# Spreading the value steps of the second stick-breaking group over three slots of a two-layer attention kernel

## The chip, the cores and the metric

The kernel runs on one core of a Trainium2 chip. The metric is the device time of one execution in microseconds, taken as the median over several runs; lower is better.

## The reference

The program is an encoder trunk of two layers (DEPTH = 2) on 512 tokens of width 1024. Each layer projects the residual stream once and feeds two mixers of eight heads each: group A, stick-breaking attention, and group B, sparse attention over each query's top 128 keys. The change touches the values of group A alone:

```python
def hybrid_layer(x, w_in, w_out, ln_g, ln_b, rel_bias, topk):
    proj = jnp.einsum('bsd,dn->bsn', x, w_in)
    qA, kA, vA, gA, qB, kB, vB, gB, qI, kI, wI = jnp.split(proj, SPLIT_POINTS, axis=-1)
    oA = stick_breaking_attention(heads(qA), heads(kA), heads(vA))
    oB = dsa_sparse_attention(heads(qB), heads(kB), heads(vB), ..., rel_bias, topk)
    mix = jnp.concatenate([oA * jax.nn.silu(gA), oB * jax.nn.silu(gB)], axis=-1)
    return layer_norm(ALPHA * x + jnp.einsum('bsm,md->bsd', mix, w_out), ln_g, ln_b)

# stick_breaking_attention, for s < t:
#   A[t,s] = sigmoid(z[t,s]) * prod_{s<j<t} (1 - sigmoid(z[t,j]));  out = A @ v
```

## The kernel before

Every product of float32 operands is made of three products of halves: a high half (a rounded copy made by ScalarE) and a low half (the source minus the high half, made by VectorE or GpSimd). So every operand that TensorE reads has such a pair of steps behind it. `XH`, `XL` are the halves of the layer's input; `whi`, `wlo` those of a weight piece. A weight piece `raw` is loaded by a transfer that SyncE issues, copied to `whi` by ScalarE in one instruction (L212) and subtracted to `wlo` by GpSimd in four or two (L215). Two `raw` buffers and four `whi`/`wlo` pairs turn over.

A layer is a loop over 91 slots (`s`). A slot starts one task, a block of 128 queries of one head: tasks 0 to 23 are the indexer's, 24 to 55 those of the eight stick heads (four blocks of a head, with 128, 256, 384 and 512 keys, in turn), then those of group B. A stick task goes through stages in consecutive slots: its logits `z` (TensorE, L517 and L520) and the sigmoid `om` (ScalarE, L704) in its own slot; a scan along the keys (VectorE, L709) one slot later; the transposes into `tr` (TensorE, L525), the high copy into one `AT` tile (ScalarE, L714) and the low copy into another (VectorE, L717) three slots later. When the four blocks of a head have been through that, the slot after the last one runs the eight matmuls of the head's output `o` (L692), which read the two `AT` tiles and the values `vt`. Its second reads are of the low tile. The output is then copied and added up (`mixt`, L594 and L596) and multiplied into `M` by GpSimd (L597). Between these, TensorE is filled with projection matmuls (`pj`, L266 to L268, and `pjv`), ahead of their use, by a table of slots by which each unit must be done. VectorE also runs the top-k rounds (L841, L842) in the same slots, and the gates' products (`sig`, L581 and L584), which GpSimd multiplies into `M` (L582, L585).

The order of the instructions on each engine is the order in which the code is written: PE, ACT, DVE and POOL each run their own list in that order and wait at an instruction until its inputs are there.

The scan makes the sum of a stick head a sum over differences of neighbouring value rows. So the values of a group go through extra steps: the projection is copied to `V_NOW`, shifted by one row into `V_PREV` by three transfers, then VectorE subtracts (L329, in place, the whole 128 x 1024; the trace names both tiles `M`, in which they lie), and the result is split into `vt`: two high copies on ScalarE (L346) and two low subtractions on VectorE (L344), each of half the token blocks.

These steps wait in a list `pending`. At the end of each slot `run_pending` takes one from every entry's count and runs entries from the front of the list while the front one's count is below zero. For the second stick group (heads 4 to 7, tasks 40 to 55), `project_v` appends an entry with count `SHIFT_SLOTS[1]` = 2, which calls `value_steps`. It falls due at the end of slot 41, in both layers. The first group's steps are called from elsewhere and the change leaves them alone. The values of the second group are read first by `o` of its first head, in slot 47. The `o` that runs in slot 43, soon after the steps, belongs to the last head of the first group and reads the other `vt`.

Of the kernel before, what the change touches and what calls it, by code (L numbers as in the profile page):

```python
# [102 lines left out]
def tile_hybrid(ctx: ExitStack, tc: tile.TileContext, xt, x, w_in, w_ki, w_out, ln_g, ln_b, rel_bias, onehot, out, depth=DEPTH):  # L103
# [182 lines left out]
    def project_v(l, unit, vt, keys=None):  # L286
# [9 lines left out]
        for tb in range(NTB):  # L296
            if tb:
                stream.want = i + min(tb + 1, 3) + (keys is not None)
            full = ppj.tile([P, S], F32, tag="pj", name="pjv")[:, :n]
            acc = full[:, :W256]  # L300
            for kc in range(KC):
                whi, wlo = (t[:, kc % 4, :] for t in w[kc // 4])
                T.matmul(full, XH[:, tb, kc, :], whi, start=kc == 0, stop=False)  # L303
                T.matmul(full, XL[:, tb, kc, :], whi, start=False, stop=False)  # L304
                T.matmul(full, XH[:, tb, kc, :], wlo, start=False, stop=kc == KC - 1)  # L305
                if kc == KC - 1:
                    if keys is not None:
                        later.append(lambda tb=tb, full=full: keep_keys(tb, full))
                    if unit[0] == "A":
                        later.append(lambda tb=tb, acc=acc: A.activation(V_NOW[:, tb, :], acc, AF.Copy))  # L310
                    else:
                        later.append(lambda tb=tb, acc=acc: evac_v(vv, tb, acc))
                if (tb, kc) == (NTB - 1, KC - 1) and unit[0] == "A":
                    later.append(shift_values)
                    pending.append([SHIFT_SLOTS[1], lambda: value_steps(vv)])
                yield 324 * n // W256
# [3 lines left out]
    pending = []  # L320
# [7 lines left out]
    def value_differences(engine, tbs=slice(0, NTB)):  # L328
        engine.tensor_tensor(V_PREV[:, tbs], V_PREV[:, tbs], V_NOW[:, tbs], ALU.subtract)  # L329

    def value_parts(vv):
        for i in range(4):
            value_part(vv, *divmod(i, 2))

    def value_steps(vv):
        value_differences(V)
        value_parts(vv)

    def value_part(vv, low, half):
        t = slice(2 * half, 2 * half + 2)  # L340
        src = V_PREV[:, t].rearrange("p t (h d) -> p t h d", d=HD)
        hi, lo = vv[:, t, :, :HD], vv[:, t, :, HD:]
        if low:
            V.tensor_tensor(lo, src, hi, ALU.subtract)  # L344
        else:
            A.activation(hi, src, AF.Copy)  # L346
# [785 lines left out]
```

## Time and profile before

| | before |
|---|---|
| median of 3 runs | 640.04 us (640.04 to 640.9) |
| the profiled execution | 639.84 us |
| its span, first to last instruction | 638.0 us |
| TensorE (PE) busy | 626.1 us, 98% |
| weight loads (PEld) busy | 546.7 us, 86% |
| VectorE (DVE) busy | 486.8 us, 76% |
| GpSimd (POOL) busy | 363.3 us, 57% |
| ScalarE (ACT) busy | 343.0 us, 54% |
| granted TensorE clock | 0.998 |

The profile gives, for each engine, the instructions in order of time, each with its start, its duration, its line and its tiles, and in brackets how long the engine had been idle before it and what ended that. The chain of waits is followed back from the last instruction to what released each step. Times in it count from the start of the span. Starts and ends on one engine can overlap by up to a tenth of a microsecond, and the ends of matmuls are modelled. The steps that the change moves lie near 135 us (layer 0) and near 449 us (layer 1).

### The profile page before, as it was taken

The page shows a single profiled execution, that of the slowest core. Times are in us where ns is not written, and L with a number is a line of the kernel's source. Part 1 is how long each engine was busy: PE and PEld are TensorE (multiplying, and loading weights), DVE is VectorE, ACT ScalarE, POOL GpSimd, SP SyncE. Part 2 cuts the span into 40 slices and gives each one's busy share as a digit, 9 for nine tenths or more (in the row PEclk, how much of TensorE's full clock was granted, in tenths as well). Part 3 has the DMA queues.
Part 4 walks back from the last instruction along what each step waited for, and adds up shares of the span by engine and source line. Part 5 has one row for each costly group of instructions (what it writes and reads, how often), then busy time and mean ns, then how long its engine had stood idle before and what let it go on. Part 6 is the DMA issues. An engine that isn't in the chain of part 4 may idle for free.

```text
span 638.0 us, 10261 instructions
## 1 busy us (share of the span) xinstructions
PE 626.1 (98%) x3501; PEld 546.7 (86%) x3501; DVE 486.8 (76%) x1058; ACT 343.0 (54%) x686; POOL 363.3 (57%) x380
## 2 busy tenths in 40 slices
PE   8999999999999999999999999999999999999995
PEld 7988888978889889988899888899788898898884
DVE  3778999988965775667845789999988576666677
ACT  5686555444357466883135855454444566678700
POOL 5463544448466676798134545535574587778721
PEclk9999999999999999999999999999999999999999
DMA  7624243312253475363314343333123724734402
GB/s 246 203 78 133 99 132 100 92 46 96 99 157 92 125 190 169 113 197 118 133 67 131 107 126 99 105 95 125 40 100 113 167 86 121 186 126 138 172 33 99
DMA packets 31779, 77.41 MB, mean 121 GB/s; under 512 B 6572, under 2 KB 10668, under 8 KB 31728
## 3 DMA queue, kind: packets, MB, share of 16 engines
q1 hardware_dynamic: 31440, 76.51, 39.0%
q8 instruction: 27, 0.44, 0.3%
q10 hardware_dynamic: 288, 0.26, 0.1%
q14 instruction: 24, 0.20, 0.1%
HBM read 61.84 MB, written 4.44 MB: 104 GB/s over the span
## 4 chain that ended last, share of the span: by engine, by line
PE 93%; DVE 3%; ACT 2%; issue 1%; DMA 1%; SPq 0%; POOL 0%; DVEq 0%; ACTq 0%
PE pj L266 15%; PE pj L267 15%; PE pj L268 15%; PE pjo L796 13%; PE o L692 6%; PE tr L525 5%; PE pjv L303 4%; PE pjv L304 4%; PE pjv L305 4%; PE z L520 4%; PE z L517 4%; PE pjv L427 2%; PE pjq L429 1%; PE trx L1050 1%; DMA q_raw<-in_w_in_dram 1%
## 5 line engine op out<-in xcount | busy, mean ns | idle before, releaser
L215 POOL TENSOR_TENSOR wlo<-raw,whi 128x256 fp32r<-128x256 f32 (+1 forms) x250 | 222.9, 922 | 162.2 <-ACT whi L212 161.4
L266 PE MATMUL pj<-XH,whi 128*128 128x512 f32 (+1 forms) x432 | 171.5, 397 | 0.0
L267 PE MATMUL pj<-XL,whi 128*128 128x512 f32 (+1 forms) x432 | 166.4, 385 | 0.0
L268 PE MATMUL pj<-XH,wlo 128*128 128x512 f32 (+1 forms) x432 | 166.2, 385 | 0.0
L268 PEld LDWEIGHTS pj<-XH,wlo 128*128 128x128 f32 x432 | 81.1, 188 | 16.1
L267 PEld LDWEIGHTS pj<-XL,whi 128*128 128x128 f32 x432 | 81.4, 188 | 12.2
L266 PEld LDWEIGHTS pj<-XH,whi 128*128 128x128 f32 x432 | 81.3, 188 | 12.2
L704 ACT ACTIVATE om<-z 128x128 f32<-128x128 f32 (+1 forms) x64 | 28.0, 438 | 111.5 <-PE z L520 61.1
L212 ACT ACTIVATE whi<-raw 128x1024 fp32r<-128x1024 f32 x78 | 81.9, 1055 | 7.4 <-DMA raw<-in_w_in_dram 7.0
L597 POOL TENSOR_TENSOR M<-M,mixt 64x512 f32<-64x512 f32 x24 | 40.6, 1691 | 51.6 <-DVE mixt L596 45.2
L709 DVE TENSOR_TENSOR_SCAN om<-om,future 128x128 f32<-128x128 f32 (+1 forms) x64 | 63.3, 988 | 0.2
L303 PE MATMUL pjv<-whi,XH 128*128 128x256 f32 x192 | 56.9, 296 | 0.0
L305 PE MATMUL pjv<-wlo,XH 128*128 128x256 f32 x192 | 54.2, 283 | 0.0
L304 PE MATMUL pjv<-whi,XL 128*128 128x256 f32 x192 | 54.2, 282 | 0.0
L841 DVE MAX8 m<-scores 128x8 f32<-128x256 f32 (+2 forms) x96 | 52.8, 550 | 0.1
L842 DVE MATCH_REPLACE8 scores<-m,scores 128x256 f32<-128x256 f32 (+2 forms) x96 | 52.1, 543 | 0.0
L692 PE MATMUL o<-AT,vt 128*128 128x512 f32 (+4 forms) x256 | 46.7, 323 | 2.8 <-ACT AT L714 2.7
L754 ACT ACTIVATE p<-p,mn 128x128 f32<-128x128 f32 (+1 forms) x64 | 35.8, 559 | 20.2 <-DVE mn L749 19.9
L692 PEld LDWEIGHTS o<-AT,vt 128*128 128x128 f32 (+1 forms) x256 | 36.5, 182 | 7.7 <-ACT AT L714 3.5
L520 PE MATMUL z<-k,q 128*128 128x128 f32 (+3 forms) x128 | 41.7, 326 | 0.0
L796 PE MATMUL pjo<-whi,XH 128*128 128x512 f32 (+1 forms) x118 | 41.1, 387 | 0.0
L796 PE MATMUL pjo<-wlo,XH 128*128 128x512 f32 (+1 forms) x118 | 41.1, 384 | 0.0
(165 smaller groups left out, 1282.4 us busy)
## 6 DMA issues: line engine op xcount, KB each, us to landing
raw<-in_w_in_dram SPq DMA_DIRECT2D x66, 512.0 KB, 3.3
k<-k SPq DMA_DIRECT2D x32, 256.0 KB, 5.6
raw<-in_w_out_dram SPq DMA_DIRECT2D x14, 512.0 KB, 3.2
gbias<-f_dram SPq DMA_DIRECT2D x18, 256.0 KB, 3.3
XN<-in_x_dram SPq DMA_DIRECT2D x8, 256.0 KB
y_dram<-XN SPq DMA_DIRECT2D x4, 512.0 KB, 2.6
XN<-y_dram SPq DMA_DIRECT2D x8, 256.0 KB, 3.7
M<-M SPq DMA_DIRECT2D x4, 448.0 KB
```

Source lines behind the costliest of these rows:

```text
L212: A.activation(hi, src, AF.Copy)
L215: low = lambda lo=lo[:, c], src=src[:, c], hi=hi[:, c]: lo_engine.tensor_tensor(lo, src, hi, ALU.subtract)
L266: T.matmul(o, w[0], XH[:, tb:, kc, :], start=first, stop=False)
L267: T.matmul(o, w[0], XL[:, tb:, kc, :], start=False, stop=False)
L268: T.matmul(o, w[1], XH[:, tb:, kc, :], start=False, stop=last)
L303: T.matmul(full, XH[:, tb, kc, :], whi, start=kc == 0, stop=False)
L304: T.matmul(full, XL[:, tb, kc, :], whi, start=False, stop=False)
L305: T.matmul(full, XH[:, tb, kc, :], wlo, start=False, stop=kc == KC - 1)
L520: T.matmul(self.z[:, :nn], c, d, start=False, stop=True)
L692: T.matmul(self.o[:m, sb * P :], vt[:, sb, self.hh * P : self.hh * P + m], at_block(self.at[j], sb, sb, NTB - sb), start=n == 0, stop=n == 7)
L709: V.tensor_tensor_scan(rev, rev, future[:, S - n :][:, ::-1], 1.0, ALU.mult, ALU.max)
L796: T.matmul(acc[:, cols], mixed[:, tb, m, :], w[:, cols], start=n == 0, stop=n == len(steps) - 1)
```

## The change

`value_steps` no longer runs the four parts behind the difference in the same slot. It appends four entries to `pending`: the two high copies with count 0, the two low subtractions with count 1. The entries are appended after the counts have been taken down for that slot, so the high copies run at the end of the next slot (42) and the low subtractions at the end of the one after it (43). No instruction is added or removed.

```diff
     def value_steps(vv):
         value_differences(V)
-        value_parts(vv)
+        for i in range(4):
+            pending.append([i // 2, lambda i=i: value_part(vv, *divmod(i, 2))])
```

The rows below are the order of the programs, layer 0; layer 1 moves alike. The file after is one line longer, so its lines from 338 on count one more. On ACT, before: behind the high copy of a three-block transpose come the two high copies of the values, then the copy of a weight piece (1569), then the sigmoid of 384 keys and the high copy of the four-block transpose.

```order
L714 ACTIVATE AT_107<-tr 128x3x128
L346 ACTIVATE vt<-M 128x8x64 x2
L212 ACTIVATE whi_1569<-raw_1404 128x1024
L704 ACTIVATE om<-z 128x384
L714 ACTIVATE AT_107<-tr 128x4x128
L704 ACTIVATE om<-z 128x512
```

On ACT, after (the same weight piece is now numbered 1565):

```order
L715 ACTIVATE AT_107<-tr 128x3x128
L212 ACTIVATE whi_1565<-raw_1404 128x1024
L705 ACTIVATE om<-z 128x384
L715 ACTIVATE AT_107<-tr 128x4x128
L347 ACTIVATE vt<-M 128x8x64 x2
L705 ACTIVATE om<-z 128x512
```

The values' copies moved behind the weight copy, one sigmoid and the four-block copy. On DVE, before: the difference and both low subtractions stand in front of the scan of 256 keys and the four-block low copy into `AT_108`.

```order
L842 MATCH_REPLACE scores_503<-m_1548,scores_503 128x256
L329 TENSOR_TENSOR M<-M 128x1024
L344 TENSOR_TENSOR vt<-M,vt 128x8x64 x2
L709 SCALAR_TENSOR_TENSOR om<-om,future 128x256
L717 SCALAR_TENSOR_TENSOR AT_108<-tr,AT_107 128x4x128
L841 MAX m_1591<-scores_504 128x8
L842 MATCH_REPLACE scores_504<-m_1591,scores_504 128x384
L709 SCALAR_TENSOR_TENSOR om<-om,future 128x384
L584 TENSOR_TENSOR sig<-pj,sig 128x512
```

On DVE, after, from the instruction that now follows the difference to the low subtractions:

```order
L710 SCALAR_TENSOR_TENSOR om<-om,future 128x256
L718 SCALAR_TENSOR_TENSOR AT_108<-tr,AT_107 128x4x128
L842 MAX m_1587<-scores_504 128x8
L843 MATCH_REPLACE scores_504<-m_1587,scores_504 128x384
L710 SCALAR_TENSOR_TENSOR om<-om,future 128x384
L585 TENSOR_TENSOR sig<-pj,sig 128x512
L718 SCALAR_TENSOR_TENSOR AT_106<-tr,AT_105 128x128
L842 MAX m_1628<-scores_505 128x8
L843 MATCH_REPLACE scores_505<-m_1628,scores_505 128x512
L842 MAX m_1631<-scores_503 128x8
L843 MATCH_REPLACE scores_503<-m_1631,scores_503 128x256
L345 TENSOR_TENSOR vt<-M,vt 128x8x64 x2
```

The low subtractions moved from behind the difference to behind the next slot's last top-k rounds, and `mixt` is the next instruction behind them. The lists of PE, POOL and SP keep their order.

## The prediction

> **What bounds the kernel now.** I read the totals first, then the chain of waits, then who keeps TensorE waiting, and last the order of time on each engine around the place that these name.
>
> ```profile
> span 638.0 us, 10261 instructions
> PE 626.1 (98%) x3501; PEld 546.7 (86%) x3501; DVE 486.8 (76%) x1058; ACT 343.0 (54%) x686; POOL 363.3 (57%) x380
> PE 93%; DVE 3%; ACT 2%; issue 1%; DMA 1%; SPq 0%; POOL 0%; DVEq 0%; ACTq 0%
> PE o L692 <- ACT AT L714: 2.7, 2, 1.4
> PE idle L399 <- DVE warm L396: 1.2, 1, 1.2
> PE pjv L427 <- DVE XL L167: 0.3, 1, 0.3
> ```
>
> TensorE is busy for 98% of the span and makes 93% of the chain. So only what lets TensorE wait less shortens the run, and the last three lines, all of TensorE's waits, name one such place outside the start: twice, once in each layer, the output `o` of a head waits for the high copy into `AT`. This is the `o` of slot 43. TensorE's own rows show the price, with one `o` that doesn't wait for comparison:
>
> ```profile
> 138.37 0.27 PE L525 MATMUL tr<-ident,om 128*128 128x128 f32 x1
> 140.01 1.80 PE L692 MATMUL o<-AT,vt 128*128 128x512 f32 x8 [1.37 <-ACT AT L714]
> 141.65 0.39 PE L266 MATMUL pj<-XH,whi 128*128 128x512 f32 x1
> 156.96 1.45 PE L692 MATMUL o<-AT,vt 128*128 128x512 f32 x8
> 453.49 1.80 PE L692 MATMUL o<-AT,vt 128*128 128x512 f32 x8 [1.37 <-ACT AT L714]
> 140.73 0.77 PEld L692 LDWEIGHTS o<-AT,vt 128*128 128x128 f32 x6 [0.43 <-DVE AT L717]
> ```
>
> The engine idles 1.37 us, and the eight matmuls then take 1.80 instead of 1.45 us, because six of them wait again, for the low copy. Together 1.72 us in a layer, 3.44 us in both, are there to be had, and no more. Why the copies into `AT` are late is told by ScalarE and VectorE:
>
> ```profile
> 132.27 0.50 ACT L714 ACTIVATE AT<-tr 128x384 fp32r<-128x384 f32 x1
> 136.99 1.16 ACT L346 ACTIVATE vt<-M 128x512 fp32r<-128x512 f32 x2 [4.22 <-DVE M L329]
> 138.05 1.04 ACT L212 ACTIVATE whi<-raw 128x1024 fp32r<-128x1024 f32 x1
> 139.00 0.47 ACT L704 ACTIVATE om<-z 128x384 f32<-128x384 f32 x1
> 139.37 0.59 ACT L714 ACTIVATE AT<-tr 128x512 fp32r<-128x512 f32 x1
> ...
> 135.74 1.22 DVE L329 TENSOR_TENSOR M<-M 128x1024 f32<-128x1024 f32 x1
> 137.66 1.29 DVE L344 TENSOR_TENSOR vt<-M,vt 128x512 fp32r<-128x512 f32 x2 [0.70 <-ACT vt L346]
> 138.87 0.69 DVE L709 TENSOR_TENSOR_SCAN om<-om,future 128x256 f32<-128x256 f32 x1
> 139.99 0.69 DVE L717 SCALAR_TENSOR_TENSOR AT<-tr,AT 128x512 fp32r<-128x512 f32 x1 [0.44 <-ACT AT L714]
> ```
>
> ScalarE stands idle for 4.22 us at the values' high copies, since the difference reaches its turn on VectorE only at 135.74, behind top-k rounds. Behind those copies queue the weight copy, a sigmoid and the four-block copy, which ends at 139.96. VectorE waits 0.70 us for the high copies, and once more, 0.44 us, for the four-block copy. Its low copy ends at 140.68, and that releases the six matmuls.
>
> **The change, part by part.** Everything moved is already in the program: the two high copies (1.16 us on ScalarE) and the two low subtractions (1.29 us on VectorE). No TensorE, GpSimd or SyncE instruction changes its place in its list, but GpSimd and SyncE get work at other times.
>
> *High copies, one slot on.* The weight copy, the sigmoid and the four-block copy no longer stand behind them. The weight copy may start at 132.77 (132.27 + 0.50) and ends near 133.8. The four-block copy needs only its transposes:
>
> ```profile
> 134.72 0.60 PE L525 MATMUL tr<-ident,om 128*128 128x128 f32 x4
> ```
>
> They end at 135.32, so with the sigmoid (0.47) and the copy (0.59) the high tile is there before 136.5, two microseconds before TensorE wants it (138.4). The wait of 1.37 goes whole. The high copies then wait for the difference, and behind them stands only the sigmoid of 512 keys, whose scan is needed slots later; I cost that at nothing, its cover being these slots.
>
> *Low subtractions, two slots on.* The scan and the low copy follow the difference at once. With the durations above the low copy would end at 135.74 + 1.22 + 0.69 + 0.69 = 138.34. TensorE would not wait for it at all, and the gain is the whole 1.72 us.
>
> *What the earlier weight copy triggers.* Its four GpSimd subtractions follow at once as well, and these meet the difference:
>
> ```profile
> 133.19 1.29 POOL L582 TENSOR_TENSOR M<-M,sig 128x512 f32<-128x512 f32 x1 [2.47 <-DVE sig L581]
> 139.17 2.99 POOL L215 TENSOR_TENSOR wlo<-raw,whi 128x256 fp32r<-128x256 f32 x4 [4.68 <-ACT whi L212]
> ```
>
> Before, they ran from 139.17, after the difference. After, they start when the gate's product is done, at 133.19 + 1.29 = 134.48, and without hindrance end near 137.5; the difference comes due at 135.74, in their midst. What such a meeting costs, the trace shows:
>
> ```profile
> 39.33 1.48 DVE L329 TENSOR_TENSOR M<-M 128x1024 f32<-128x1024 f32 x1
> 341.55 3.52 POOL L215 TENSOR_TENSOR wlo<-raw,whi 128x512 fp32r<-128x512 f32 x2 [2.37 <-ACT whi L212]
> 341.59 2.32 DVE L329 TENSOR_TENSOR M<-M 128x1024 f32<-128x1024 f32 x1
> 104.73 0.94 DVE L709 TENSOR_TENSOR_SCAN om<-om,future 128x256 f32<-128x256 f32 x1
> 130.84 0.41 DVE L709 TENSOR_TENSOR_SCAN om<-om,future 128x128 f32<-128x128 f32 x1
> 164.22 2.82 POOL L215 TENSOR_TENSOR wlo<-raw,whi 128x256 fp32r<-128x256 f32 x4
> 165.11 2.22 DVE L709 TENSOR_TENSOR_SCAN om<-om,future 128x128 f32<-128x128 f32 x1
> ```
>
> The same difference takes 1.22 us alone, but 1.48 and 2.32 at the two other places, among GpSimd's subtractions; the scan of 256 keys 0.94 instead of 0.69; and one scan of 128 keys waited out a whole series of four, 2.22 instead of 0.41. So the low copy's end has two bounds: 138.34 (nothing lost, 1.72 gained), and, if the difference waits until the series has ended, 137.5 + 1.22 + 0.69 + 0.69 = 140.1 (0.6 gained). I take the rows nearest to the case, those of the difference itself: a mean loss of (0.26 + 1.10) / 2 = 0.68, and the scan at 0.94: 135.74 + 1.90 + 0.94 + 0.69 = 139.27, against 140.68 a gain of 1.41 us in a layer.
>
> The Trainium skill bears on this in "SBUF — State Buffer", section "SBUF: two separate sides": the port pair that VectorE's instructions with two SBUF inputs share with GpSimd is an exclusive lock, and the loser waits until the other's instruction is finished. By that rule the difference loses at most what is left of one GpSimd instruction, 2.82 / 4 = 0.71 us, and the scan another 0.71: the low copy would end by 139.76, a gain of 0.92 or more in a layer. The 2.32 agrees with it; the 2.22, a loss of 1.81 us to instructions of 0.71 each, goes beyond it, so the measurement keeps the lower bound at 0.6.
>
> *The next slots.* TensorE now runs ahead by up to 1.7 us, while VectorE carries the subtractions (1.29) later. Has it the room? These rows follow it to the next `o`, at 156.96 before:
>
> ```profile
> 142.90 0.66 DVE L584 TENSOR_TENSOR sig<-pj,sig 128x512 f32<-128x512 f32 x1
> 143.64 1.29 POOL L585 TENSOR_TENSOR M<-M,sig 64x512 f32<-64x512 f32 x1 [1.48 <-DVE sig L584]
> 144.99 0.61 POOL L586 COPY M<-sig 64x512 f32<-64x512 f32 x1
> 146.03 0.69 DVE L596 TENSOR_TENSOR mixt<-o,mixt 64x512 f32<-64x512 f32 x1
> 153.98 0.67 DVE L717 SCALAR_TENSOR_TENSOR AT<-tr,AT 128x512 fp32r<-128x512 f32 x1
> 158.30 0.69 DVE L588 TENSOR_TENSOR M<-pj,sig 128x512 f32<-128x512 f32 x1 [1.66 <-ACT sig L579]
> ```
>
> VectorE comes out of the four-block low copy 1.41 us earlier and pays 1.29 us in front of `mixt`: from 146.03 on it stands where it stood. Its low copy for the next `o` ends at 154.65; TensorE would be there at 156.96 - 1.41 = 155.55. So 0.9 us of room are left of 2.31, and at 158.30 VectorE has 1.66 us of idle time to catch up in. GpSimd's product and copy (1.29 + 0.61) end before the low subtractions begin and leave them undisturbed. SyncE's next weight load follows the end of GpSimd's series, which comes some 3 us earlier; earlier loads harm nothing. The load behind it is tied to GpSimd's next series, which waits for `mixt` and so stays where it was.
>
> *Sum.* Two layers by 1.41 is 2.82 us: 639.84 - 2.8 = 637.0 for the profiled execution. The median of the runs lies 0.2 us above that execution, so 637.2. The ends: two by 1.72, 636.6; two by 0.6, 638.8. A fifth of a per cent, 1.3 us, is about what a measurement of this kernel tells from no change: 638.76 is the bound of faster.
>
> **The rivals.**
>
> *Whole gain* (nothing lost on the port): 636.6. For it speaks that TensorE needs the low half only for the third matmul, which forgives some 0.4 us more. The meeting with GpSimd's series at 134.48 to 137.5 speaks against it. Chance 0.2.
>
> *Given back at the next output.* The wait moves to the `o` near 155.5. It decides when VectorE's low copy ends more than 0.9 us later than at 154.65, or when the difference waits out the series and a scan does too. Between 149 and 155 GpSimd runs two series in a row, and a scan that came into their midst could lose 1.8 us as at 165.11; then 0.9 of the 1.41 is lost in that layer, and in both 1.0 us is left of the gain: 639.0. Speaking against it: of the scans in this stage only that one in each layer lost so much. Chance 0.16.
>
> *Slower.* If the low subtractions themselves meet a GpSimd series and each waits it out, VectorE is 2 x 1.81 = 3.6 us late at `mixt`; the next `o` then waits 3.6 - 0.9 = 2.7 us, and the layer loses 2.7 - 1.4 = 1.3, the run 2.6: 642.6. It decides from 2.3 us of lateness on. Against it stands that GpSimd's next series can't begin before `mixt`, which comes after the subtractions. Chance 0.06.
>
> *Nothing moved:* the values' parts would have to stay behind some older entry of the list. The order of the after program shows them moved, so this has no chance of its own.
>
> **How the numbers follow.** The forecast case, between 0.6 and 1.6 us a layer, has 0.58, of which 0.03 falls short of faster; with the whole gain that is 0.75 for faster. Of the giving back, 0.15 ends within the measurement's bound and 0.01 beyond it on the slow side; with that remainder no difference has 0.18 and slower 0.06 + 0.01 = 0.07. The range reaches from 636.4 (the whole gain, less a quarter of a microsecond for the spread of runs) to 639.4 (the giving back, with as much above) and leaves out the slower case and some of the edges.
>
> **What would show it.** In the profile after, the waits of TensorE lose the two of `o` for `AT` or keep them at a few tenths, now for the low copy; ScalarE's wait at the weight copy near 132.8 is gone, its weight copy stands at 132.7 and the four-block copy before 136.5; GpSimd's four subtractions start at 134.5 and the difference takes between 1.4 and 2.4 us; the low subtractions follow the top-k rounds near 144.7 and the `o` near 155.5 starts without a wait. I am wrong if that `o` waits, if VectorE's scans near 150 grow by over a microsecond, or if TensorE's idle time vanishes at 140 and the span doesn't follow.

## The result and the profile after

The median fell from 640.06 to 635.75 us, 4.3 us or 0.7%: the ratio of the runs is 0.9928, with a 95% interval of 0.9914 to 0.9943. The direction was forecast; the time lies 0.65 us below the low end of the range, and the gain is one and a half times the 2.8 us that were forecast. The profiled execution took 635.70 us, with a span of 633.9.

First the totals, the chain and TensorE's waits, as shown of before. (Lines from 338 on count one more.)

```profile
span 633.9 us, 10261 instructions
PE 624.9 (99%) x3501; PEld 547.0 (86%) x3501; DVE 486.9 (77%) x1058; ACT 343.2 (54%) x686; POOL 364.1 (57%) x380
PE 92%; POOL 2%; ACT 2%; DMA 1%; DVE 1%; issue 1%; SPq 0%; DVEq 0%; POOLq 0%; ACTq 0%
PE idle L400 <- DVE warm L397: 1.2, 1, 1.2
PE pjv L428 <- DVE XL L167: 0.2, 1, 0.2
PE pjv L428 <- DVE AT L437: 0.2, 1, 0.2
```

The two waits of `o` for `AT` are gone, and nothing has come in their place: all that TensorE still waits for lies in the first ten microseconds. The place itself, in order of time, on TensorE, ScalarE, VectorE and GpSimd (start, duration, and in brackets the idle time before):

```profile
138.26 0.27 PE L526 MATMUL tr<-ident,om 128*128 128x128 f32 x1
138.29 1.47 PE L693 MATMUL o<-AT,vt 128*128 128x512 f32 x8
139.59 0.39 PE L266 MATMUL pj<-XH,whi 128*128 128x512 f32 x1
...
132.54 1.07 ACT L212 ACTIVATE whi<-raw 128x1024 fp32r<-128x1024 f32 x1
135.25 0.60 ACT L715 ACTIVATE AT<-tr 128x512 fp32r<-128x512 f32 x1
136.89 1.15 ACT L347 ACTIVATE vt<-M 128x512 fp32r<-128x512 f32 x2 [1.04 <-DVE M L329]
...
135.63 1.22 DVE L329 TENSOR_TENSOR M<-M 128x1024 f32<-128x1024 f32 x1
136.78 1.23 DVE L710 TENSOR_TENSOR_SCAN om<-om,future 128x256 f32<-128x256 f32 x1
137.93 0.66 DVE L718 SCALAR_TENSOR_TENSOR AT<-tr,AT 128x512 fp32r<-128x512 f32 x1
...
134.34 4.19 POOL L215 TENSOR_TENSOR wlo<-raw,whi 128x256 fp32r<-128x256 f32 x4
```

The four-block high copy ends at 135.85 instead of 139.96, the low copy at 138.59 instead of 140.68, and `o` follows the transpose at once. From the start of the transpose to the start of the next projection it is 139.59 - 138.26 = 1.33 us; before it was 141.65 - 138.37 = 3.28. So 1.95 us have gone here, and not 1.72. In layer 1 the same two starts stand at

```profile
449.83 0.27 PE L526 MATMUL tr<-ident,om 128*128 128x128 f32 x1
451.17 0.39 PE L266 MATMUL pj<-XH,whi 128*128 128x512 f32 x1
```

1.34 us apart. When each TensorE instruction's start after is set against its start before, the difference is a staircase of two steps: -0.1 us from the start on, -2.06 behind the `o` of layer 0, -2.02 ahead of the `o` of layer 1, -3.96 behind it, and between -4.1 and -4.2 at the end. But for 0.04 us between the layers, nothing of the gain is given back. At the next `o`, VectorE's copy is early:

```profile
152.77 0.66 DVE L718 SCALAR_TENSOR_TENSOR AT<-tr,AT 128x512 fp32r<-128x512 f32 x1
154.90 1.45 PE L693 MATMUL o<-AT,vt 128*128 128x512 f32 x8
```

It ends 1.47 us before `o` starts, where 0.9 had been worked out.

### The profile page after: what moved, and what is told of

It reads as the page before. It is cut to its first block, busy times and chain, and to the rows that moved or that the text cites. A ratio compares the mean times of both kernels' runs of the same rounds, so it can differ in the third digit from the quotient of the medians.

```text
span 633.9 us, 10261 instructions
## 1 busy us (share of the span) xinstructions
PE 624.9 (99%) x3501; PEld 547.0 (86%) x3501; DVE 486.9 (77%) x1058; ACT 343.2 (54%) x686; POOL 364.1 (57%) x380
## 4 chain that ended last, share of the span: by engine, by line
PE 92%; POOL 2%; ACT 2%; DMA 1%; DVE 1%; issue 1%; SPq 0%; DVEq 0%; POOLq 0%; ACTq 0%
PE pj L266 15%; PE pj L267 15%; PE pj L268 15%; PE pjo L797 12%; PE o L693 5%; PE tr L526 5%; PE z L521 4%; PE pjv L303 4%; PE z L518 4%; PE pjv L304 4%; PE pjv L305 4%; PE pjv L428 2%; POOL wlo L215 1%; PE pjq L430 1%; ACT p L755 1%
## 5 line engine op out<-in xcount | busy, mean ns | idle before, releaser
L537 DVE TENSOR_TENSOR AT<-tr,AT 128x128 fp32r<-128x128 f32 (+1 forms) x64 | 31.2, 488 | 11.5 <-ACT AT L534 11.2
```

## The experiments

The question was where the 1.5 us beyond the forecast come from, and which of the moved steps pays. Theory A: all of the gain is the wait of that one output, it is 1.95 us a layer, and it hangs on the two four-block copies, first on ScalarE's. The experiments ran on two occasions, beside runs of before with a median of 639.83 (first four) and 639.96 us (last four). Line numbers below count by each run's own file.

**One layer alone.** `value_steps` gets a flag: in layer 1 the parts run at once as before (the flag's own lines in `value_steps` are left out here).

```diff
-    pending.append([SHIFT_SLOTS[1], lambda: value_steps(vv)])
+    pending.append([SHIFT_SLOTS[1], lambda: value_steps(vv, l == 0)])
```

> The steps are spread in layer 0 only; layer 1 keeps them in one slot. Theory A (all of the gain is the wait of the output in slot 43, 1.96 us a layer counted from the start of the transpose to the start of the next projection, 3.28 - 1.32): half of the gain, 2.0 to 2.2 us faster than before, about 638.0. Rival B (the 0.7 us beyond the 3.44 us that the idle rows allowed are a gain elsewhere, not tied to a layer): 1.7 us from the layer plus 0.7, about 637.6. In the trace A wants the TensorE shift against before to stay at -2.0 us from 142 us to the end.

Measured: 637.91 us, 1.92 less than before, ratio 0.9969 (0.9958 to 0.9981). TensorE's one remaining wait of this kind is that of layer 1:

```profile
PE o L696 <- ACT AT L718: 1.4, 1, 1.4
```

The difference of starts against before steps from about 0.0 to -1.91 at that `o` and then stays between -1.7 and -2.0 to the end, except at single starts. Theory A holds: the gain comes in two equal parts. Rival B's 637.6 lies close by in time, but its 0.7 us elsewhere don't show.

**Low subtractions alone.** The high copies stay right behind the difference.

```diff
-        for i in range(4):
-            pending.append([i // 2, lambda i=i: value_part(vv, *divmod(i, 2))])
+        for i in range(2):
+            value_part(vv, 0, i)
+        for i in range(2):
+            pending.append([1, lambda i=i: value_part(vv, 1, i)])
```

> Only the low subtractions are moved (two slots behind the difference); the high copies stay right behind it on ScalarE. Theory A (ScalarE's list is the cause: its four-block copy stands behind high copies that wait for the difference): the four-block copy still ends near 139.9, the low copy waits for it, gain 0.0 to 0.2 us, about 640.0. Rival C (VectorE's list is the cause, by the 1.29 us of subtractions and the 0.70 us wait in front of the low copy): 1.0 to 2.0 us a layer, 636.0 to 638.0.

Measured: 640.05 us, ratio 1.0001 (0.9992 to 1.0010): nothing. ScalarE, VectorE and TensorE there (this execution ran 0.4 us later from the start on):

```profile
137.40 1.15 ACT L349 ACTIVATE vt<-M 128x512 fp32r<-128x512 f32 x2 [4.22 <-DVE M L329]
139.78 0.59 ACT L717 ACTIVATE AT<-tr 128x512 fp32r<-128x512 f32 x1
137.28 0.68 DVE L712 TENSOR_TENSOR_SCAN om<-om,future 128x256 f32<-128x256 f32 x1
140.39 0.69 DVE L720 SCALAR_TENSOR_TENSOR AT<-tr,AT 128x512 fp32r<-128x512 f32 x1 [2.43 <-ACT AT L717]
140.41 1.80 PE L695 MATMUL o<-AT,vt 128*128 128x512 f32 x8 [1.36 <-ACT AT L717]
```

VectorE is rid of the subtractions and done with the scan at 137.96, but then stands for 2.43 us until ScalarE's copy is there, and TensorE waits as before. The time that was freed turned into a wait. Rival C falls: the high copies' place on ScalarE is what has to change first. The high copies alone were not moved in any run, since the low subtractions read them and can't run ahead of them.

**Both one slot behind.**

```diff
-            pending.append([i // 2, lambda i=i: value_part(vv, *divmod(i, 2))])
+            pending.append([0, lambda i=i: value_part(vv, *divmod(i, 2))])
```

> High copies and low subtractions both run one slot behind the difference. Theory A: the low subtractions are already behind the four-block low copy there, so the whole gain, 4.0 to 4.3 us, about 635.8, and no difference to the changed kernel. Rival D (the second slot of distance is needed, since the subtractions now stand in front of the scan of 384 keys and the gate's product): 0.5 us or more of the gain is lost, 636.3 or above.

Measured: 635.93 us, ratio 0.9937 (0.9924 to 0.9949). That is 3.90 us less than before, 0.1 short of what was expected, and as much as the changed kernel gained when it was measured again (below). The second slot of distance does nothing that shows; rival D, at 636.3 or above, falls.

**In one piece, one slot later.** The kernel before with one number changed.

```diff
-SHIFT_SLOTS = (4, 2)
+SHIFT_SLOTS = (4, 3)
```

> The kernel before, its value steps in one piece as they were, but due one slot later (at the end of slot 42 in place of 41). Theory A (only what stands between slot 41 and the output in slot 43 on ScalarE and VectorE counts): the difference comes behind the four-block copies, and TensorE doesn't wait: the whole gain, 4.0 to 4.3 us, about 635.8. Rival E (it is the spreading that pays: in one piece the steps hold up ScalarE wherever they stand, here the sigmoid of 512 keys and the copy of the output): the wait moves one head on, and 1 us or more a layer is lost, 637.8 or above.

Measured: 635.82 us, ratio 0.9935 (0.9922 to 0.9947), 4.01 us less than before: the whole gain again. On ScalarE, VectorE and TensorE:

```profile
135.43 0.60 ACT L714 ACTIVATE AT<-tr 128x512 fp32r<-128x512 f32 x1
139.37 1.15 ACT L346 ACTIVATE vt<-M 128x512 fp32r<-128x512 f32 x2 [3.34 <-DVE M L329]
136.43 0.66 DVE L717 SCALAR_TENSOR_TENSOR AT<-tr,AT 128x512 fp32r<-128x512 f32 x1
138.47 1.46 PE L692 MATMUL o<-AT,vt 128*128 128x512 f32 x8
```

ScalarE still stands idle at the high copies, for 3.34 us, and nobody minds: both four-block copies are done by 137.1, and what is queued behind the high copies now is not wanted soon. So it is not the spreading that pays, and not the idle time of ScalarE, but the place of the steps against the `o` of slot 43. Rival E falls.

**How much room is left.** The changed kernel with one, then two, more maxima of 512 scores on VectorE ahead of the low copy; the result isn't used.

```diff
+                if self.head.i == 0 and self.head.hh == 3 and self.qb == NTB - 1:
+                    for _ in range(1):      # 2 in the second kernel
+                        V.max(sm.tile([P, 8], F32, tag="m83", name="m8", bufs=2), scores[NTB - 1])
                 V.scalar_tensor_tensor(self.blocks(at[1]), ...)
```

> The changed kernel with one more top-k maximum of 512 scores (0.68 us, result unused) on VectorE, right ahead of the four-block low copy that the output in slot 43 reads, in both layers. Theory A (that low copy, ended at 138.59, is just in time: before, the next projection began 0.97 us after its end, and 139.59 - 0.97 = 138.62, so 0.03 us of room): TensorE loses 0.6 us a layer, 1.1 to 1.4 us in all, about 637.0. Rival F (TensorE forgives some 0.4 us more, as the prediction held): 0.3 us a layer, about 636.3.

> The same with two such maxima (1.4 us). Theory A: 1.3 us a layer, 2.4 to 2.8 us in all, about 638.4. Rival F: 0.95 us a layer, about 637.7.

The changed kernel itself ran beside them:

> The changed kernel itself, beside the three others on one chip: 4.0 to 4.3 us faster than before, to read their differences from.

Measured: the changed kernel 636.06 us, ratio 0.9937 (0.9924 to 0.9949), a gain of 3.90 us where 4.0 to 4.3 had been expected; with one maximum 637.27, with two 638.47. That is 1.21 and 2.41 us more, 0.60 us a layer for each. TensorE's waits, of the first and of the second kernel:

```profile
PE o L693 <- DVE AT L721: 0.6, 2, 0.3
```

```profile
PE o L693 <- DVE AT L721: 1.8, 2, 0.9
```

Each maximum costs in full (0.6 us is its pitch, since rows overlap by a tenth), from the first one on. So the low copy of the changed kernel is just in time, without room to speak of. Its end, 138.59, lies 0.30 us behind the start of `o`, since the first two weight loads of `o` read the high tile alone. The third, the first to read the low tile, starts at 138.64. Rival F, 0.4 us of forgiveness on top of that, falls.

**Without the meeting of GpSimd and VectorE.** The changed kernel, with ScalarE's weight copy held back by one slot:

```diff
-            stream.prep_ahead()
+            if s != 41:
+                stream.prep_ahead()
```

> The changed kernel with the weight copy of slot 41 held back on ScalarE by one slot, so that GpSimd's four subtractions don't meet the difference and the scan. Theory A (the meeting lengthened the scan by 0.54 us, but the low copy was still in time): the scan of 256 keys takes 0.69 again, the low copy ends near 138.05, and the time is that of the changed kernel within 0.3 us, about 635.8. Rival G (the meeting on the port costs what the prediction took off, 0.3 us a layer or more): faster than the changed kernel by 0.6 us or more, 635.2 or below.

Measured: 635.94 us, 0.12 less than the changed kernel beside it, whose runs spread from 635.55 to 636.29. VectorE's rows:

```profile
135.57 1.22 DVE L329 TENSOR_TENSOR M<-M 128x1024 f32<-128x1024 f32 x1
136.70 0.69 DVE L710 TENSOR_TENSOR_SCAN om<-om,future 128x256 f32<-128x256 f32 x1
137.30 0.67 DVE L718 SCALAR_TENSOR_TENSOR AT<-tr,AT 128x512 fp32r<-128x512 f32 x1
```

The scan takes 0.69 again and the low copy ends at 137.97, 0.6 us before the changed kernel's, which TensorE can't use: it comes to the `o` no earlier. The meeting costs no time that shows. It eats the room that the low copy would otherwise have had. Rival G falls. The run did not rid the kernel of every such meeting: the low subtractions of the values now meet the gate's product on GpSimd (L586) and take 2.4 us in either layer instead of 1.3, and TensorE doesn't wait for that either.

## Why the prediction was wrong

The place, the cause and the direction were right: the high copies held up ScalarE's four-block copy, the wait of `o` vanished, and no wait took its place. Most of the rows that were named came as named: the weight copy at 132.5 (132.7 said), the four-block copy done by 135.9 (before 136.5), GpSimd's series from 134.34 (134.5), no wait at the `o` near 155. One did not: the difference was to take between 1.4 and 2.4 us and took 1.22. The low subtractions start at 143.5 rather than 144.7, since VectorE had got through earlier. Two terms of the sum were mis-sized.

*The ceiling, "Together 1.72 us in a layer, 3.44 us in both, are there to be had, and no more".* It was put together from the idle time of 1.37 and the longer duration of 0.35. The idle time counts from the end that the profile gives the transpose, 138.37 + 0.27 = 138.64. But an `o` that doesn't wait starts 0.03 us after the start of the transpose, as 156.96 in the prediction's own row follows a transpose at 156.93:

```profile
156.93 0.27 PE L525 MATMUL tr<-ident,om 128*128 128x128 f32 x1
158.25 0.39 PE L266 MATMUL pj<-XH,whi 128*128 128x512 f32 x1
```

From start to start this unhindered head takes 1.32 us and the hindered one took 3.28: 1.96 us a layer, 3.92 in all. The two profiles show it, and the run with one layer alone shows half of it. With the ceiling at 1.72 not even the rival that loses nothing could come below 636.6 us; 635.75 were measured.

*The meeting with GpSimd's series, 0.93 us a layer.* The difference was charged a mean loss of 0.68 from its two other places and lost nothing; the scan was charged 0.25 and lost 0.54. The low copy so ended at 138.59 and not at 139.27, 2.09 us earlier than before instead of 1.41, which is just enough for the whole 1.95. What went wrong is the mean. At the places from which it was taken the difference had come 0.40 and 1.24 us ahead of the end of the GpSimd instruction then under way, and lost 0.26 and 1.10. Here it came 0.14 us ahead of such an end and lost nothing, which the prediction had not foreseen. That the gain came whole was luck as far as the prediction goes. The last section has the rows. The rule of the Trainium skill that the prediction weighed ("SBUF — State Buffer", "SBUF: two separate sides") had bounded the low copy's end at 139.76, with a loss of up to one GpSimd instruction for each of the two; both losses, 0.0 and 0.54, lie within it.

Of the 0.54 us a layer that the forecast fell short of the 1.95, the meeting makes 1.72 - 1.41 = 0.31 and the ceiling the rest. In both layers that is 2 x (1.95 - 1.41) = 1.08 of the 1.5 us. Of the remaining 0.4 us, a quarter of a microsecond is the -0.1 at the start and what came on in the last stage, and the rest is that the medians lie 4.31 us apart and the profiled executions 4.14. Nothing shows that this is tied to the change: at 20 us the starts of the nine other executions lie between -0.27 and +0.41 us from those of before, and the second measurement of the changed kernel gives a gain of 3.9 us, where two waits of 1.95 make 3.9.

The rival of the whole gain (chance 0.2) is what happened, at a price that the false ceiling had cut to 3.44 us. Its reason was right in part: the low half did come 0.30 us after `o` had started, and `o` did not wait. But this is no allowance beyond the 1.95: it is used up, as the two runs with added maxima show. The giving back at the next output and the slower case didn't come: no scan near 150 grew (0.69 and 0.68 us, where before they took 0.70 and 0.68), and the low subtractions met no series. A slip without weight is the upper end of the range: as much above 639.0 as the lower end has below 636.6 is about 639.25 and not 639.4.

## What to carry to other kernels

Size a stall of TensorE from start to start, against an unhindered copy of the same piece of the program, and not from the idle time that stands beside a row: where matmuls overlap, that idle time is short by the overlap, here by 0.24 of 1.96 us, and an upper bound built on it is false. On an engine that runs a list in order, an instruction that waits for a late input should stand behind what the bound engine will ask for next; here one number that moved three steps by one slot did as much as spreading them over three. Freed time on one of two engines in a chain is worth nothing while the other one still ends last. And a meeting of two engines is priced from where in the other's instruction it falls, not from a mean over other places.

## What the runs showed of the hardware

What VectorE's differences and scans, which read two tiles in SBUF, lose to a series of subtractions on GpSimd depends on how far the GpSimd instruction under way has got. The rows below are from the traces of before and after; times in us.

| VectorE's instruction | its start | GpSimd's instruction ends | left of it | lost |
|---|---|---|---|---|
| difference, before | 39.33 | 39.73 | 0.40 | 0.26 |
| difference, before | 341.59 | 342.83 | 1.24 | 1.10 |
| scan of 128 keys, before | 84.85 | 85.53 | 0.68 | 0.55 |
| scan of 256 keys, before | 104.73 | 105.13 | 0.40 | 0.25 |
| difference, after | 135.63 | 135.77 | 0.14 | 0.00 |
| scan of 256 keys, after | 136.78 | 137.45 | 0.67 | 0.54 |

The loss is what was left, less 0.13 to 0.15 us. The ten traces have some 350 such meetings, and about nine in ten agree with this within 0.03 us. In the changed kernel the two engines got their turns one after the other: GpSimd's third subtraction was held up by the difference, the scan by that third subtraction, and the fourth by the scan.

```profile
135.03 0.74 POOL L215 TENSOR_TENSOR wlo<-raw,whi 128x256 fp32r<-128x256 f32 x1
135.73 1.72 POOL L215 TENSOR_TENSOR wlo<-raw,whi 128x256 fp32r<-128x256 f32 x1
137.42 1.11 POOL L215 TENSOR_TENSOR wlo<-raw,whi 128x256 fp32r<-128x256 f32 x1
```

GpSimd's four took 4.19 us where they had taken 2.99 before. The same meeting came out alike at all eleven places where the runs have it: the difference lost at most 0.01 us. So the term that the prediction took from a mean could have been estimated from the trace of before. There the last three of the four subtractions start 0.70 us apart and take 0.74 each. In a series from 134.48 the second ends at 134.48 + 0.70 + 0.74 = 135.92, 0.18 us after the difference comes due at 135.74, and by the rows above that costs some 0.04 us.

There are two kinds of exception. Where the two instructions started within 0.07 us of one another, it was in some places GpSimd's that waited (the scan of 512 keys at 97.41 before lost nothing). And a scan of 128 keys a few slots on waited out its whole series, as before:

```profile
162.22 2.80 POOL L215 TENSOR_TENSOR wlo<-raw,whi 128x256 fp32r<-128x256 f32 x4
163.10 2.20 DVE L710 TENSOR_TENSOR_SCAN om<-om,future 128x128 f32<-128x128 f32 x1
```

Here it lost 1.8 us and GpSimd nothing. The ten traces have this scan twenty times, always with 0.52 to 0.55 us left of GpSimd's instruction. Sixteen times it took 2.20 to 2.22 us; four times, in the runs with one layer alone (layer 0), with two maxima (layer 1) and with the weight copy held back (both layers), it took 0.80 to 0.85. So it is not how far GpSimd has got that makes this case; what does was not tried and stays open.
